# Setting the high and the low part of each channel block side by side in one tile

## The chip, the cores and the metric

The kernel runs on one core of one Trainium2 chip. The metric is the device time of one execution in microseconds (us). Three runs of the kernel before gave 1538.27, 1538.55 and 1540.19 us; their median, 1538.55 us, is the time that the change is measured against.

## The reference

Two stacks of layers are applied one after the other to one sequence of 256 tokens with 1024 channels, all in float32. The part that matters here is that nearly all the work is products of a normalised input with a weight matrix:

```
def first_block(x, ...):                 # 2 layers
    x = hybrid_layer(x, ...)             # h = rmsnorm(x); proj = h @ w_in (1024 x 2304)
                                         # two attentions; y = [rmsnorm(ya), rmsnorm(yb)]
                                         # x = x + y @ w_out (1024 x 1024)
                                         # u = rmsnorm(x) @ w_mlp_in (1024 x 4096); u = relu(u)^2
                                         # x = x + u @ w_mlp_out (4096 x 1024)
    return rmsnorm(x, final_norm)

def second_block(x, ...):                # 2 layers
    f = swiglu(x, w_gate, w_up, w_down)  # 1024 x 2816, 1024 x 2816, 2816 x 1024
    x = layer_norm(ALPHA * x + 0.5 * f)
    z = x @ w_in                         # 1024 x 2304, then three mixers
    x = layer_norm(ALPHA * x + y @ w_out)
    f = swiglu(x, ...); x = layer_norm(ALPHA * x + 0.5 * f)
```

## The kernel before

The channels lie across the 128 partitions in 8 blocks (`KT` = 8) and the 256 tokens in two tiles of 128 (`NT` = 2). A float32 product is made of three products of float32r operands: each operand is split into a high part (a copy rounded to float32r) and a low part (the remainder), and `mm3` (L165) adds high x high, high x low and low x high into one PSUM tile. So every line L166, L167 and L168 stands for one matmul of a triple.

A normalised input is kept transposed, with channels on partitions: `new_xT` (L103) gives two tiles, `xh` for the high and `xl` for the low part, each with 8 blocks of 256 tokens. `padded` (L73) makes such a tile 24 elements (96 bytes per partition) longer than its contents. The pool `xtp` has two buffers of each name, so that there are four tiles: `xh`, `xh`, `xl`, `xl`. The same pair holds the mixed output `yT` of an attention or of the mixers before its projection.

These tiles are written in pieces: by `transpose_to` and `split` (L224, L220: four blocks of 128 tokens in one instruction), by `rms_in` (L265 and L266: one block each), by `values` (L413 and L414: one block of 256 tokens) and in `mixers` by `split` from SBUF (two blocks of 256 tokens, L784 and L811). ACT writes the high part and DVE the low part.

They are read in three forms:

- `b_form` (L176): the weights, `whi` and `wlo`, are loaded into the array as the stationary operand, 128 columns at a time, and a whole block of `xh` or `xl` (256 tokens) streams through as the moving operand. One pass is 8 blocks x 3 matmuls = 24 matmuls of 256 columns.
- `a_form` (L170): `xh` or `xl` (128 tokens) is the stationary operand and 256 columns of `whi` or `wlo` stream. It is used in `layer1` throughout and elsewhere for the first units of a stage.
- `out_form` (L186): the stationary operand is a hidden activation in tiles of the name `six`, or `yT` in `xh` and `xl`; 512 columns of the weights stream.

The weights come by DMA into `wraw` (L148) and are split at L153 into `whi` (ACT) and `wlo` (DVE), with eight buffers each. Every stage begins with `enter` (L206), which sets the transposes of the new input between the last products of the stage before and the first of its own. The order of the attention stages is written out in `ORDER` (L39); in the rest it is the order of the code.

Of the kernel before, what the change touches and what calls it, by code (L numbers as in the profile page):

```python
# [12 lines left out]
F32R = mybir.dt.float32r  # L13
# [6 lines left out]
P = 128  # L20
S = 256
NT = 2
D = 1024
KT = 8
# [21 lines left out]
def hybrid_stack(ctx: ExitStack, tc: tile.TileContext, a, out):  # L46
# [7 lines left out]
    xtp = ctx.enter_context(tc.tile_pool(name="xtp", bufs=2))  # L54
# [15 lines left out]
    def T(pool, shape, tag, dt=F32, **kw):  # L70
        return pool.tile(shape, dt, tag=tag, name=nm(tag), **kw)

    def padded(pool, shape, tag, dt, **kw):  # L73

        n = shape[1] * shape[2]
        t = T(pool, [P, n + 24], tag, dt, **kw)
        return t[:, :n].rearrange("p (a b) -> p a b", b=shape[2])
# [23 lines left out]
        return [[acc1() for _ in range(2)] for _ in range(NT)]  # L101

    def new_xT():  # L103
        return padded(xtp, [P, KT, S], "xh", F32R), padded(xtp, [P, KT, S], "xl", F32R)

    def chunks():
        return [(c, slice(c * 512, (c + 1) * 512)) for c in range(2)]
# [336 lines left out]
    def layer1(l, xT, rx, boundary):  # L444
# [12 lines left out]
        kTB = T(m4k, [P, 4, S], "m4k")  # L457
        ssum = [T(tmp, [P, S], "ti", bufs=2) for _ in range(2)]
        yT = new_xT()
        rqA = T(tiny, [P, 16], "rqA", bufs=1).rearrange("p (t h) -> p t h", t=NT)  # L460
        held = {}
# [232 lines left out]
    def mixers(l, xT, boundary):  # L694
# [27 lines left out]
        for t in range(NT):  # L722
            alpha_x(t)
        yT = new_xT()


# [93 lines left out]
    acc, finish, r = None, None, None  # L820
    for l in range(DEPTH):
        xT = new_xT()
        if l == 0:
            tab = T(const, [P, NT, 160], "tab")
# [24 lines left out]
        xT = new_xT()  # L849
# [10 lines left out]
    xT = new_xT()  # L860
# [4 lines left out]
    def ln_stage(l, i, acc, scale):  # L865
        g, b = gain(a["ln_g_2"][l, i]), gain(a["ln_b_2"][l, i], tag="b")
        xT = None if (l, i) == (DEPTH - 1, 2) else new_xT()

        def f(t):
            ln_xT(x[t], acc[t], scale, g, b, xT, t, out[0, t * P:(t + 1) * P, :] if xT is None else None)  # L870

        return f, xT

    for l in range(DEPTH):
        acc, finish = ffn(l, 0, xT, (finish, norm))
        norm, xT = ln_stage(l, 0, acc, 0.5)
        acc, finish = mixers(l, xT, (finish, norm))
        norm, xT = ln_stage(l, 1, acc, 1.0)
        acc, finish = ffn(l, 1, xT, (finish, norm))
        norm, xT = ln_stage(l, 2, acc, 0.5)  # L880
# [73 lines left out]
```

## Time and profile before

| | |
|---|---|
| median of three runs | 1538.55 us |
| the profiled execution's own time | 1543.87 us |
| its span, first to last instruction | 1542.1 us |
| granted TensorE clock, mean over the span | 0.997 |
| busy: PE, PEld, DVE, ACT, POOL | 98%, 90%, 66%, 53%, 4% of the span |
| DMA | 177 GB/s in the mean |

PE stands for the matmuls, PEld for the loads of the stationary operand, which overlap with them; DVE, ACT and POOL are the engines for vector, scalar and general work. The matmuls are pipelined: the duration shown for one (some 280 ns for 256 columns) is longer than the distance between the starts of two, so what a matmul costs is read from the length of a stretch divided by the matmuls that begin in it. The profiled execution took 1.8 us outside its span.

### The profile page before, as it was taken

What the parts mean: (1) busy time and instruction counts of PE and PEld (TensorE: products, weight loads), DVE (VectorE), ACT (ScalarE), POOL (GpSimd) and SP (SyncE); (2) the same over time, 40 slices, a digit from 0 to 9 for tenths busy, and PEclk for the clock granted to TensorE, in tenths of its full rate; (3) what the DMA queues carried; (4) which work ended last, traced back from release to release, by engine and by line L of the source; (5) the groups of instructions that cost most, each with busy time, mean ns of one, the idle gap of its engine ahead of it and who ended that gap; (6) DMA issues with size and microseconds to landing.
All of it is one profiled execution on the core that took longest, in us unless ns stands there. A gap on an engine that the chain in (4) does not pass through costs nothing. (4 is left out here: it accounts for less than half of the span.)

```text
span 1542.1 us, 26996 instructions
## 1 busy us (share of the span) xinstructions
PE 1511.1 (98%) x10480; PEld 1390.8 (90%) x10480; DVE 1016.2 (66%) x2056; ACT 817.1 (53%) x1636; POOL 64.7 (4%) x94
## 2 busy tenths in 40 slices
PE   7999999999999999999999999999999999999998
PEld 6889999889899998999999899998999999899997
DVE  7977656589775555655577875556755477875554
ACT  6866554478574544544446554443644447454441
POOL 3000000030000000000000100000000000000000
PEclk9999999999999999999999999999999999999999
DMA  6624665635366654866646576664866646476661
GB/s 194 191 68 152 214 195 181 191 98 169 108 194 183 194 184 137 252 189 185 189 134 219 157 231 182 190 190 137 253 191 191 186 134 214 150 242 186 188 186 47
DMA packets 196368, 272.98 MB, mean 177 GB/s; under 512 B 9312, under 2 KB 169600, under 8 KB 196240
## 3 DMA queue, kind: packets, MB, share of 16 engines
q1 hardware_dynamic: 193664, 262.76, 55.6%
q0 software_dynamic: 2576, 8.50, 1.9%
q8 instruction: 82, 1.34, 0.4%
q14 instruction: 46, 0.38, 0.1%
HBM read 270.17 MB, written 1.05 MB: 176 GB/s over the span
## 5 line engine op out<-in xcount | busy, mean ns | idle before, releaser
L153 DVE TENSOR_TENSOR wlo<-wraw,whi 128x512 fp32r<-128x512 f32 x992 | 641.0, 687 | 363.6 <-ACT whi L153 354.6
L153 ACT CAST whi<-wraw 128x512 fp32r<-128x512 f32 x992 | 565.5, 619 | 530.6 <-issue 267.5
L166 PE MATMUL rot<-xh,whi 128*128 128x256 f32 x1088 | 306.3, 282 | 0.0
L167 PE MATMUL rot<-xl,whi 128*128 128x256 f32 x1088 | 306.1, 281 | 0.0
L168 PE MATMUL rot<-xh,wlo 128*128 128x256 f32 x1088 | 304.5, 280 | 0.0
L167 PE MATMUL aux<-xl,whi 128*128 128x256 f32 x864 | 242.5, 281 | 0.0
L166 PE MATMUL aux<-xh,whi 128*128 128x256 f32 x864 | 242.1, 280 | 0.0
L168 PE MATMUL aux<-xh,wlo 128*128 128x256 f32 x864 | 241.8, 280 | 0.0
L166 PE MATMUL acc<-whi,six 128*128 128x512 f32 x608 | 240.8, 396 | 0.2 <-ACT six L221 0.2
L168 PE MATMUL acc<-whi,six 128*128 128x512 f32 x608 | 238.8, 394 | 0.0
L167 PE MATMUL acc<-wlo,six 128*128 128x512 f32 x608 | 238.6, 393 | 0.0
L167 PEld LDWEIGHTS rot<-xl,whi 128*128 128x128 f32 x1088 | 204.6, 188 | 0.7
L166 PEld LDWEIGHTS rot<-xh,whi 128*128 128x128 f32 x1088 | 204.6, 188 | 0.6
L168 PEld LDWEIGHTS rot<-xh,wlo 128*128 128x128 f32 x1088 | 204.6, 188 | 0.1
L166 PEld LDWEIGHTS aux<-xh,whi 128*128 128x128 f32 x864 | 162.5, 188 | 2.1
L167 PEld LDWEIGHTS aux<-xl,whi 128*128 128x128 f32 x864 | 162.3, 188 | 2.2
L168 PEld LDWEIGHTS aux<-xh,wlo 128*128 128x128 f32 x864 | 162.5, 188 | 0.0
L166 PE MATMUL rot<-whi,xh 128*128 128x256 f32 x544 | 156.5, 288 | 0.6 <-ACT qk L719 0.5
L167 PE MATMUL rot<-wlo,xh 128*128 128x256 f32 x544 | 154.5, 284 | 0.8 <-DVE wlo L153 0.8
L168 PE MATMUL rot<-whi,xl 128*128 128x256 f32 x544 | 154.5, 286 | 0.1
L168 PEld LDWEIGHTS acc<-whi,six 128*128 128x128 f32 x608 | 114.1, 188 | 28.0 <-DVE six L222 1.0
L166 PEld LDWEIGHTS acc<-whi,six 128*128 128x128 f32 x608 | 114.2, 188 | 24.2 <-ACT six L221 1.7
(215 smaller groups left out, 1721.2 us busy)
## 6 DMA issues: line engine op xcount, KB each, us to landing
wraw<-in_ffn_w_gate_dram SPq DMA_DIRECT2D x88, 512.0 KB, 4.5
wraw<-in_ffn_w_up_dram SPq DMA_DIRECT2D x88, 512.0 KB, 4.4
wraw<-in_ffn_w_down_dram SPq DMA_DIRECT2D x88, 512.0 KB, 4.4
wraw<-in_w_in_dram SPq DMA_DIRECT2D x71, 512.0 KB, 4.6
wraw<-in_w_mlp_in_dram SPq DMA_DIRECT2D x64, 512.0 KB, 4.5
wraw<-in_w_mlp_out_dram SPq DMA_DIRECT2D x64, 512.0 KB, 4.5
wraw<-in_w_out_dram SPq DMA_DIRECT2D x32, 512.0 KB, 4.0
g<-in_ln_g_dram POOLq DMA_DIRECT2D x6, 512.0 KB, 4.1
```

Source lines behind the costliest of these rows:

```text
L153: done[:] = [se.copy(h, r), ve.tensor_tensor(l, r, h.bitcast(F32), op=ALU.subtract)]
L166: pe.matmul(o, lh, rh, start=first, stop=False)
L167: pe.matmul(o, lh, rl, start=False, stop=False)
L168: pe.matmul(o, ll, rh, start=False, stop=last)
```

## The change

`new_xT` now makes one tile, `xT`, of 16 blocks of 256 elements, and gives its even blocks as the high and its odd blocks as the low part:

```
     def new_xT():
-        return padded(xtp, [P, KT, S], "xh", F32R), padded(xtp, [P, KT, S], "xl", F32R)
+
+        xT = padded(xtp, [P, 2 * KT, S], "xT", F32R).rearrange("p (k i) s -> p k i s", i=2)
+        return xT[:, :, 0], xT[:, :, 1]
```

Nothing else is edited; lines behind L104 have a number higher by two. On every engine the built program has the same instructions in the same order, with the same waits. Two things differ.

First, the places. Within a partition the tiles before start at bytes 104768 and 113056 (`xh`) and 121344 and 129632 (`xl`), which is 320, 416, 512 and 608 bytes past a multiple of 1024; all of `whi` and `wlo` start 320 bytes past one. The new tiles start at 104768 and 121248, and the low block of a pair 1024 bytes behind the high one, so that high and low both lie 320 bytes past a multiple of 1024 in the first buffer and both 416 in the second. Since there are two pads fewer, every tile of the pools opened behind `xtp` starts 192 bytes earlier: the five `six` buffers were 0, 96, 192, 288 and 384 bytes past a multiple of 1024 and are now 832, 928, 0, 96 and 192. Tiles of pools opened earlier, `wraw`, `whi` and `wlo` among them, stay where they were.

Second, the shape of twelve writes. The two blocks that `split` writes in one instruction in `mixers` were adjacent and counted as one run of 512 elements; now a low block stands between them. On ACT, in the mixers of the first layer of the second block, where `whi` is a weight's high part and `m4k` and `six` are results of the mixers, there stood before:

```order
L774 COPY six_9869<-rot_9954 128x512 [waits PE_49]
L153 CAST whi_10173<-wraw_10172 128x512
L221 CAST xh_9488<-m4k_9491 128x512 [waits DVE_49,Activation_49]
L221 CAST xh_9488<-m4k_9491 128x512 [waits DVE_49]
L153 CAST whi_10181<-wraw_10180 128x512 [waits DMAHW2_49,PE_49]
L153 CAST whi_10181<-wraw_10180 128x512
```

and now:

```order
L776 COPY six_9860<-rot_9945 128x512 [waits PE_49]
L155 CAST whi_10164<-wraw_10163 128x512
L223 CAST xT_9480<-m4k_9482 128x2x256 [waits DVE_49,Activation_49]
L223 CAST xT_9480<-m4k_9482 128x2x256 [waits DVE_49]
L155 CAST whi_10172<-wraw_10171 128x512 [waits DMAHW2_49,PE_49]
L155 CAST whi_10172<-wraw_10171 128x512
```

The two casts write two runs of 256 in place of one of 512, at the same place in ACT's order and behind the same waits; a third cast some instructions later, and DVE's three subtractions for them, change in the same way, in each of the two layers.

On PE, at the first product of the program, the triple read two tiles:

```order
L166 MATMUL rot_227<-whi_162,xh_109 128x256 [waits Activation_49]
L262 MATMUL aux_271<-ident_99,x_188 128x128
L167 MATMUL rot_227<-wlo_163,xh_109 128x256 [waits DVE_49]
L168 MATMUL rot_227<-whi_162,xl_110 128x256
L166 MATMUL rot_227<-whi_162,xh_109 128x256
```

and reads one now:

```order
L168 MATMUL rot_225<-whi_160,xT_109 128x256 [waits Activation_49]
L264 MATMUL aux_269<-ident_99,x_186 128x128
L169 MATMUL rot_225<-wlo_161,xT_109 128x256 [waits DVE_49]
L170 MATMUL rot_225<-whi_160,xT_109 128x256
L168 MATMUL rot_225<-whi_160,xT_109 128x256
```

No matmul moved, and none waits for anything that it did not wait for before.

## Rows read from the trace of the kernel before

**Rows 1.** The page: span, busy time by engine, granted clock in 40 slices.
```profile
span 1542.1 us, 26996 instructions
...
PE 1511.1 (98%) x10480; PEld 1390.8 (90%) x10480; DVE 1016.2 (66%) x2056; ACT 817.1 (53%) x1636; POOL 64.7 (4%) x94
...
PEclk9999999999999999999999999999999999999999
```

**Rows 2.** The page: the chain that ended last, by engine.
```profile
DVE 0%; DVEq 0%; issue 0%
```

**Rows 3.** Waits of PE, the two longest: us in total, times, longest.
```profile
PE aux L262 <- DMA x<-in_x_dram: 9.3, 2, 5.0
PE aux L355 <- DVE four L222: 2.8, 2, 2.0
```

**Rows 4.** Groups by form: count, busy us and mean ns, idle before.
```profile
L153 DVE TENSOR_TENSOR wlo<-wraw,whi 128x512 fp32r<-128x512 f32 x992 | 641.0, 687 | 363.6 <-ACT whi L153 354.6
L153 ACT CAST whi<-wraw 128x512 fp32r<-128x512 f32 x992 | 565.5, 619 | 530.6 <-issue 267.5 <-PE rot L167 91.9 <-PE acc L168 79.1
L166 PE MATMUL rot<-xh,whi 128*128 128x256 f32 x1088 | 306.3, 282 | 0.0
...
L166 PE MATMUL aux<-xh,whi 128*128 128x256 f32 x864 | 242.1, 280 | 0.0
...
L166 PE MATMUL acc<-whi,six 128*128 128x512 f32 x608 | 240.8, 396 | 0.2 <-ACT six L221 0.2
...
L166 PE MATMUL rot<-whi,xh 128*128 128x256 f32 x544 | 156.5, 288 | 0.6 <-ACT qk L719 0.5
...
L166 PE MATMUL acc<-whi,xh 128*128 128x512 f32 x128 | 51.9, 405 | 0.0
```

**Rows 5.** PE by window, matmuls reading `xh`: length, busy (count), clock, DMA share, GB/s.
```profile
704.77:716.08 11.31, 11.31 (x64) 1.00 0.60 185
926.75:938.05 11.31, 11.31 (x64) 1.00 0.61 191
```

**Rows 6.** PE by window, matmuls writing `acc`: four groups of 24 with `six`.
```profile
171.80:177.31 5.51, 5.51 (x24) 1.00 0.72 210
194.16:199.75 5.59, 5.59 (x24) 1.00 0.65 196
182.97:188.51 5.54, 5.54 (x24) 1.00 0.70 215
...
536.61:542.10 5.50, 5.50 (x24) 1.00 0.70 212
```

**Rows 7.** PE by window, matmuls writing `acc`: two groups of 24 with `yT`.
```profile
862.25:867.84 5.58, 5.58 (x24) 1.00 0.71 224
...
1323.16:1328.71 5.55, 5.55 (x24) 1.00 0.75 229
```

**Rows 8.** PE by window, matmuls writing `rot`: three passes of `a_form`.
```profile
68.76:71.59 2.83, 2.83 (x26) 1.00 0.39 146
65.85:68.76 2.91, 2.91 (x24) 1.00 0.73 218
379.11:381.88 2.77, 2.77 (x26) 1.00 0.03 6
```

**Rows 9.** Groups by form: writes of `xh` and `xl` by `split`.
```profile
L222 DVE TENSOR_TENSOR xl<-aux,xh 128x512 fp32r<-128x512 f32 x24 | 15.7, 686 | 2.4 <-ACT xh L221 2.3
...
L221 ACT CAST xh<-aux 128x512 fp32r<-128x512 f32 x24 | 14.1, 588 | 59.6 <-PE aux L227 58.7
...
L222 DVE TENSOR_TENSOR xl<-m4k,xh 128x512 fp32r<-128x512 f32 x4 | 2.6, 682 | 0.0
...
L221 ACT CAST xh<-m4k 128x512 fp32r<-128x512 f32 x4 | 2.3, 621 | 2.1 <-DVE m4k L810 2.1
...
L222 DVE TENSOR_TENSOR xl<-aux,xh 128x256 fp32r<-128x256 f32 x4 | 1.7, 421 | 0.1
...
L221 ACT CAST xh<-aux 128x256 fp32r<-128x256 f32 x4 | 1.5, 366 | 0.0
```

## The prediction

> **What bounds the kernel now.** I read the page first. Its busy shares show one engine that never rests: PE is busy for 1511.1 of 1542.1 us, DVE for 66% and ACT for 53% [rows 1]. The granted clock stands at nine tenths or more in each of the 40 slices [rows 1], so the clock hides nothing and has nothing to give back; it is at the upper of its two levels, 2.4 GHz. The chain that ended last has 0% for each engine that it names [rows 2], because it only follows the last few microseconds of the program; it is no guide here, and I went to the waits instead. PE's longest waits are 9.3 us for the first load of `x` and 2.8 us in an attention [rows 3]. In the groups the idle time ahead of the matmuls is between 0.0 and 0.6 us over hundreds of instructions, while DVE and ACT wait hundreds of microseconds ahead of the weights' splits [rows 4]. So the kernel takes as long as PE needs to work off its matmuls one after the other, and the only question about a change is whether it makes a matmul start later after the one before it.
>
> **What a matmul costs** is the length of a stretch divided by the matmuls in it. Two stretches of four `b_form` passes, one on the first and one on the second buffer of the input, both take 11.31 us [rows 5]. The rows count 64 matmuls that read `xh`; with one on `xl` for every two of these it is 96, so 11.31 / 96 = 117.8 ns each. With `six` as the loaded operand, 24 matmuls of 512 columns take 5.50, 5.51, 5.54 or 5.59 us [rows 6], which is 229.2 to 232.9 ns each; with `yT` 5.55 and 5.58 us [rows 7]. A pass of `a_form` takes 2.83, 2.91 or 2.77 us for the 24 matmuls that begin in it (the rows' counts take in the tail of a neighbour) [rows 8].
>
> The counts come from the groups, three lines to a form [rows 4]: `b_form` has 3 x (1088 + 864) = 5856 matmuls, or 690 us; `a_form` 3 x 544 = 1632, which is 68 passes, or 192 us; `out_form` with `six` 3 x 608 = 1824, which is 76 groups of 24, or 421 us at 5.54; with `yT` 3 x 128 = 384, which is 16 groups, or 89 us. These are 1392 of the 1542 us.
>
> **The change, part by part.** Instructions, order and waits are the same on every engine, so nothing is removed, added or queued behind something else. No DMA of a weight lands elsewhere. What remains is where operands lie.
>
> *Twelve writes in two runs.* In the mixers six casts on ACT take 621 ns and six subtractions on DVE 682 ns for one run of 512 [rows 9]. The nearest rows are the same two lines writing four runs of 128: 588 and 686 ns [rows 9], so runs by themselves cost nothing on either engine (the first reads from another memory, so I use it for the order of size only). The far bound is that two runs of 256 cost as much as two instructions of 256: 2 x 366 = 732 and 2 x 421 = 842 ns [rows 9], which is 6 x 0.11 + 6 x 0.16 = 1.6 us in all. I take the four-run rows, hence 0. Even the far bound would lie beside PE's work: before the casts of weights ACT is idle for 530.6 us in total and DVE for 363.6 us [rows 4]. With that cover gone it would be +1.6 us.
>
> *`b_form`.* The weights are loaded and the input streams. The loaded operand stays at its place. What streams moves: a low block lay 512 or 608 bytes past a multiple of 1024 and now lies 320 or 416 past one, as the high block does and did. The two buffers before differ in just this, by 96 bytes in both parts, and their stretches agree to the last digit shown, 0.01 us in 11.31 [rows 5]. So I take 0, with 61 such stretches x 0.01 = 0.6 us to either side as far as offsets like those seen go.
>
> *`out_form` with `six`.* Here the loaded operand moves by 192 bytes, and this is where the trace does show a dependence: the groups of [rows 6] have the same code, the same engines and the same clock, and differ in which of the five buffers hold the high and the low part. The fast ones, 5.51 and 5.50 us, have the high part at offset 0 and the low at 384; the slow one, 5.59, at 192 and 0; the one between, 5.54, at 288 and 96. DMA traffic does not explain it, since a fast and a slow group have 210 and 196 GB/s. The change gives all five buffers new offsets, so each pair draws anew. I find no rule in the rows that tells good offsets from bad ones: 288 and 96 are as far apart as 192 and 0. The middle of the ends, 5.545, is my value before and after, so 0; the ends are 76 x 0.045 = 3.4 us either way.
>
> *`a_form` and `yT`.* The loaded operand is `xh` or `xl`. Its low part moves from 512 or 608 to 320 or 416. Of the three passes the usual one is 2.83; 2.91 is the first pass behind transposes, in either buffer, and I read it as their tail rather than as an offset; 2.77 is rare. I take 2.83, so 0. The ends are 68 x 0.06 = 4.1 us down and, if 2.91 were an offset after all, 68 x 0.08 = 5.4 us up. For `yT` it is 16 x 0.03 = 0.5 us.
>
> The sum is 0. With all ends at once it is -8.6 or +11.5 us, but these are draws for ten or so pairs of buffers and three forms, and they partly cancel; a third of the ends, -3 to +4 us, is my own range for the sum.
>
> **A rule of the Trainium skill against these rows.** The Trainium skill, in "TensorE: Matmul & The Clock Gate", section "Back-to-back issue gap", gives N / 2.4 + 2.5 ns between matmuls of N columns, and in "What happens when you issue a matmul" it says that the loads have a read port of their own, so that they take nothing from the running matmul. By that, as an estimate from this page, 256 and 512 columns would take 109 and 216 ns and no offset could matter; the sum would be 0 with no ends at all. The trace disagrees in both: 117.8 ns [rows 5], and 229.2 to 232.9 ns by buffer [rows 6]. I go by the rows, which leave the sum where it is and give it its ends.
>
> **From the profiled execution to the median.** The rows are of an execution of 1542.1 us span and 1543.87 us in all, 5.3 us above the median of 1538.55. A difference of 0 carries over to the median as it is: **1538.5 us**. A measurement of this kernel tells a difference from none at about 0.2%, which is 3.1 us.
>
> **The rivals.**
>
> *Slower: high, low and weights in step.* In the first buffer every streamed block and every loaded block of `b_form` now have the same offset, 320, and in the second 416 against 320, without exception. If PE reads the streamed and the loaded operand from one memory and they get in each other's way when in step, the third of `b_form` that streams `xl` would pay. The price from the rows is the slow against the fast group, (5.59 - 5.50) / 24 = 3.75 ns [rows 6]; 1952 matmuls x 3.75 ns = +7.3 us, hence 1545.9 us. It decides from the point where a stretch of 96 takes over 11.36 us (+3.1 us over 61 stretches). Against it speaks that in the first buffer before two of three matmuls were in step already, in the second none, and both took 11.31 us [rows 5]. I give it 0.10; together with a bad draw of `six` and `a_form` by over 3.1 us, slower has 0.15.
>
> *Faster: a good draw.* If most pairs of `six` land where 5.50 is, that is -3.4 us, and if equal offsets of high and low bring `a_form` to 2.77, -4.1 us [rows 6, 8]; both are 1531.0 us, and one of them with a little of the other some 1534.5 us. For it: two of the four groups in the rows are already at 5.50. Against it: these are averages over many pairs, and a pair that is fast now loses its place too. I give it 0.12.
>
> *The change does not do what it says*, because high and low part in one tile might be taken for one piece of memory, with reads of the one waiting for writes of the other. The PE rows of the order show no wait added, and PE waits 0.0 us at nearly all triples [rows 4]; under 0.01.
>
> **How the numbers follow.** No change beyond 0.2% has 0.73, faster 0.12, slower 0.15. The forecast's own range is 1535.5 to 1542.5 us. To leave out no more than two in ten I reach to the near edge of both draws, 1534.5 and 1543.0 us; the in-step case at 1545.9 stays outside.
>
> **What would show it.** Right: a `b_form` stretch of four passes at 11.31 us in both buffers, twelve writes near 621 and 682 ns, groups with `six` still between 5.50 and 5.59 us but in another order of buffers, `a_form` passes at 2.83. Wrong: a `b_form` stretch off 11.31 by 0.05 or more, since 5856 matmuls hang on it; all groups of `six` at one end; or a new wait of PE of over 3 us.

## The result, and the profile after

The changed kernel takes 1551.14 us in the median of six runs, the kernel before, in six runs too, 1540.04 us. The ratio is 1.0073, with a 95% interval of 1.0061 to 1.0084: 11.1 us slower, outside the range of the prediction.

On the page of the profile after, the span and PE's busy time answer to [rows 1]:

```profile
span 1549.4 us, 26996 instructions
...
PE 1521.8 (98%) x10480; PEld 1402.2 (91%) x10480; DVE 1015.7 (66%) x2056; ACT 817.0 (53%) x1636; POOL 64.6 (4%) x94
```

PE is busy for 10.7 us longer with the same number of instructions; DVE, ACT and POOL are not. The span grew by 7.3 us only, because PE idled 27.6 us in this execution and 31.0 in that of before. About half of that lies at the first transposes, on which no part of the change acts. There PE waited 9.3 us before, in two waits for the loads of `x` [rows 3]. In the waits of PE after (us in total, times, longest) the second of the two is put down to a split of a weight, and both together are 7.6 us:

```profile
PE aux L264 <- DMA x<-in_x_dram: 4.0, 1, 4.0
PE aux L264 <- DVE wlo L155: 3.6, 1, 3.6
```

Behind the first transposes no wait of PE grew by more than 0.7 us, so it is not waits that make the kernel slower. What grew is the distance between matmuls. Two stretches of four `b_form` passes, on the first and on the second buffer, with the matmuls on `xT` counted (the second count takes in the tail of a neighbour), answer to [rows 5]:

```profile
654.79:666.30 11.52, 11.52 (x96) 1.00 0.62 187
816.94:828.46 11.52, 11.52 (x98) 1.00 0.89 284
```

They took 11.31 us and take 11.52, which is 120.0 ns for a matmul in place of 117.8, at a granted clock of 1.00 as before. If all 61 stretches were like these two, it would be 61 x 0.21 = 12.8 us. Groups of 24 that write `acc` answer to [rows 6, 7]; the first three load `six`, the last two `yT`:

```profile
157.76:163.37 5.61, 5.61 (x24) 1.00 0.81 275
169.12:174.67 5.55, 5.55 (x24) 1.00 0.67 214
191.75:197.25 5.49, 5.49 (x24) 1.00 0.66 206
864.06:869.51 5.45, 5.45 (x24) 1.00 0.76 231
869.51:874.95 5.44, 5.44 (x25) 1.00 0.58 167
```

With `six` these groups spread from 5.49 to 5.61 us, about as before; with `yT`, whose parts now have equal offsets too, they became faster, 5.44 in place of 5.55 us. Passes of `a_form` answer to [rows 8]:

```profile
66.94:69.82 2.88, 2.88 (x26) 1.00 0.54 152
376.91:379.72 2.81, 2.81 (x26) 1.00 0.02 6
63.98:66.94 2.96, 2.96 (x24) 1.00 0.81 227
```

Each of these three is 0.04 or 0.05 us longer than the pass at its place before. The twelve writes in two runs answer to [rows 9], in groups by form, for eight of the twelve:

```profile
L224 DVE TENSOR_TENSOR xT<-m4k,xT 128x512 fp32r<-128x512 f32 x4 | 2.6, 684 | 0.0
L223 ACT CAST xT<-m4k 128x512 fp32r<-128x512 f32 x4 | 2.3, 621 | 1.9 <-DVE m4k L812 1.9
```

They take 684 and 621 ns, as one run did (682 and 621).

### The profile page after: what moved, and what is told of

It is laid out like the page before. It is cut to its first block, busy times and chain, and to the rows that moved or that the text cites. A ratio compares the mean times of both kernels' runs of the same rounds, so it can differ in the third digit from the quotient of the medians.

```text
span 1549.4 us, 26996 instructions
## 1 busy us (share of the span) xinstructions
PE 1521.8 (98%) x10480; PEld 1402.2 (91%) x10480; DVE 1015.7 (66%) x2056; ACT 817.0 (53%) x1636; POOL 64.6 (4%) x94
## 5 line engine op out<-in xcount | busy, mean ns | idle before, releaser
L168 PE MATMUL rot<-xT,whi 128*128 128x256 f32 x1088 | 308.6, 284 | 0.0
L169 PE MATMUL rot<-xT,whi 128*128 128x256 f32 x1088 | 308.0, 283 | 0.0
L170 PE MATMUL rot<-xT,wlo 128*128 128x256 f32 x1088 | 307.1, 282 | 0.0
L169 PE MATMUL aux<-xT,whi 128*128 128x256 f32 x864 | 244.2, 283 | 0.0
L170 PE MATMUL aux<-xT,wlo 128*128 128x256 f32 x864 | 244.0, 282 | 0.0
L168 PE MATMUL aux<-xT,whi 128*128 128x256 f32 x864 | 243.8, 282 | 0.0
L169 PEld LDWEIGHTS rot<-xT,whi 128*128 128x128 f32 x1088 | 206.1, 189 | 0.8
L168 PEld LDWEIGHTS rot<-xT,whi 128*128 128x128 f32 x1088 | 206.2, 190 | 0.6
L170 PEld LDWEIGHTS rot<-xT,wlo 128*128 128x128 f32 x1088 | 206.3, 190 | 0.1
L168 PEld LDWEIGHTS aux<-xT,whi 128*128 128x128 f32 x864 | 163.9, 190 | 2.2
L169 PEld LDWEIGHTS aux<-xT,whi 128*128 128x128 f32 x864 | 163.6, 189 | 2.2
L170 PEld LDWEIGHTS aux<-xT,wlo 128*128 128x128 f32 x864 | 164.0, 190 | 0.0
L168 PE MATMUL rot<-whi,xT 128*128 128x256 f32 x544 | 156.1, 287 | 0.5 <-ACT qk L721 0.5
L169 PE MATMUL rot<-wlo,xT 128*128 128x256 f32 x544 | 154.2, 284 | 0.7 <-DVE wlo L155 0.6
L170 PE MATMUL rot<-whi,xT 128*128 128x256 f32 x544 | 154.2, 285 | 0.7 <-DVE xT L268 0.6
```

Of the source, the lines that this page charges most:

```text
L168: pe.matmul(o, lh, rh, start=first, stop=False)
L169: pe.matmul(o, lh, rl, start=False, stop=False)
L170: pe.matmul(o, ll, rh, start=False, stop=last)
```

## The experiments

Theory 1 was that `b_form` is slow because the high and the low block, which stream one after the other, have the same offset. Its rivals were the neighbourhood (one tile, a step of 2048 bytes between blocks) and the 192 bytes by which all later tiles moved. Each stretch shown below is four passes of `b_form`, 96 matmuls, unless the text says otherwise; the count in brackets is of the matmuls on the tile named `xh` (64 of the 96) or `xT` (96).

**Equal offsets in two separate tiles.**

```
-        return padded(xtp, [P, KT, S], "xh", F32R), padded(xtp, [P, KT, S], "xl", F32R)
+        return (T(xtp, [P, KT, S], "xh", F32R), T(xtp, [P, KT, S], "xl", F32R))
```

and a filler of 384 bytes behind them.

> The kernel before with two separate tiles for high and low part, but without their pads, so that all four start 320 bytes past a multiple of 1024 and a low block has the same offset as its high block; a filler keeps every other tile where it was before. Theory 1 (equal offsets of the high and the low block that stream one after the other cost it): a stretch of 96 b_form matmuls takes 11.52 us instead of 11.31, and the kernel is about 11 us (0.7%) slower than before. Theory 2 (the neighbourhood costs it: blocks 1024 bytes apart in one tile, a step of 2048 between blocks): 11.31 us and the time of before. Theory 3 (the 192 bytes by which the other tiles moved cost it): the time of before.

It took 1550.76 us, a ratio to before of 1.0074 (1.0058 to 1.0090), and in its trace:

```profile
671.29:682.79 11.50, 11.50 (x64) 1.00 0.61 189
```

This is the change's loss without the change's layout. The neighbourhood is not needed for it.

**Side by side with 32 bytes between.**

```
-        xT = padded(xtp, [P, 2 * KT, S], "xT", F32R).rearrange("p (k i) s -> p k i s", i=2)
-        return xT[:, :, 0], xT[:, :, 1]
+        t = T(xtp, [P, KT * 520], "xT", F32R).rearrange("p (k n) -> p k n", n=520)
+        return t[:, :, 0:S], t[:, :, 264:264 + S]
```

> The changed kernel with high and low block still side by side in one tile, but with 32 bytes behind each block, so that a low block starts 1056 bytes behind its high block (32 past the same offset) and the next high block another 1024 on. Theory 1: offsets differ again, so a stretch of 96 b_form matmuls comes back to about 11.31 us and the kernel to within 0.3% of before, if 32 bytes are enough of a difference. Theory 2: still 11.5 us and about 0.7% slower than before. Theory 3: still slower, since the other tiles moved too.

It took 1543.61 us, a ratio of 1.0024 (1.0015 to 1.0033):

```profile
654.44:665.77 11.34, 11.34 (x96) 1.00 0.63 188
815.23:826.57 11.34, 11.34 (x98) 1.00 0.93 287
```

With the high and low block still neighbours in one tile, 0.18 of the 0.21 us came back, and two thirds of the time. The rest of 0.24% is not all explained by 61 x 0.03 = 1.8 us. The 32 bytes stand behind each high block only; so every pair of blocks lies 32 bytes further past a multiple of 256 than the one before it, and the tiles behind `xtp` lie 128 bytes later than in the kernel before.

**The change, with the rest in place.** A filler of 192 bytes behind `xtp`:

```
+    fill = ctx.enter_context(tc.tile_pool(name="fill", bufs=1))
+    fill.tile([P, 48], F32, tag="fill", name="fill")
```

> The changed kernel with a filler of 192 bytes behind its input tiles, so that every other tile lies where it lay before. Theories 1 and 2: nothing comes back in b_form, 11.52 us for 96 matmuls; groups of six return to 5.50 to 5.59 us as before; 0.6 to 0.8% slower than before. Theory 3: the time of before.

It took 1552.02 us, a ratio of 1.0078 (1.0061 to 1.0095), and `b_form` stays slow, so the moved tiles are not the cause:

```profile
656.21:667.71 11.50, 11.50 (x96) 1.00 0.65 187
```

One part of the expectation failed. These are the groups of 24 with `six` that stand where [rows 6] stand, with the same buffers at the same addresses as before:

```profile
170.62:176.22 5.60, 5.60 (x24) 1.00 0.71 217
181.96:187.51 5.55, 5.55 (x24) 1.00 0.70 203
193.27:198.87 5.60, 5.60 (x24) 1.00 0.71 221
```

The group that took 5.51 us before, high part at offset 0 and low at 384, takes 5.60 here. The time of such a group hangs on more than its own addresses; what differs in the matmuls ahead of it is the place of the low part in `b_form`.

**How large a difference must be.** With two tiles, the low part 128, 256, 512 or 64 bytes past the offset of the high one (a pool of its own for `xl` behind a gap of so many bytes, both parts without pads, the rest in place but for 512, where it lies 128 bytes later). The cut is of the first, without its filler and its line in `new_xT`:

```
+    gap = ctx.enter_context(tc.tile_pool(name="gap", bufs=1))
+    gap.tile([P, 32], F32, tag="gap", name="gap")
+    xlp = ctx.enter_context(tc.tile_pool(name="xlp", bufs=2))
```

> The kernel before with all high tiles 320 bytes past a multiple of 1024 and all low tiles 128 bytes further, every other tile in place. Theory 1a (only equal offsets modulo 1024 cost): 11.31 us for a stretch of 96 b_form matmuls, as with a difference of 192. Theory 1b (the offsets count modulo 128 or less): 11.52 us, as with no difference.

> The same with the low tiles 256 bytes further than the high ones. Theory 1a: 11.31 us. Theory 1b, modulo 128 or 256: 11.52 us. If 128 bytes gave 11.31 and this gives 11.52, the length is 256.

> The same with the low tiles 512 bytes further than the high ones (the tiles behind them lie 128 bytes later). Theory 1a: 11.31 us. Theory 1b, modulo 512 or a divisor of it: 11.52 us.

> The kernel before with all high tiles 320 bytes past a multiple of 1024 and all low tiles 64 bytes further. Equal offsets modulo 256 cost 11.52 us in a stretch of 96 b_form matmuls, 32, 128 and 192 bytes gave 11.31 to 11.35. If only a difference of 0 modulo 256 is bad: 11.31 us.

With 128 bytes:

```profile
634.16:645.47 11.31, 11.31 (x64) 1.00 0.82 260
```

with 256:

```profile
708.87:720.37 11.50, 11.50 (x64) 1.00 0.60 185
```

with 512:

```profile
656.64:668.15 11.50, 11.50 (x64) 1.00 0.61 188
```

and with 64:

```profile
636.06:647.37 11.31, 11.31 (x64) 1.00 0.86 261
```

The single times agree: 1537.97, 1554.52, 1552.54 and 1541.37 us, against runs of the kernel before between 1537 and 1545. Theory 1a falls, and so does 1b for 128: of the differences tried, 0, 256 and 512 are bad and 32, 64, 128 and 192 are not, so the offsets of the streamed pair count modulo 256 bytes, and 0 is the bad difference.

**Is it the streamed pair alone?** The changed kernel with the pool `wlo` 128 bytes later, so that the loaded pair `whi`, `wlo` has unequal offsets (all tiles behind, the input's among them, lie 128 bytes later too):

```
+    gapw = ctx.enter_context(tc.tile_pool(name="gapw", bufs=1))
+    gapw.tile([P, 32], F32, tag="gapw", name="gapw")
     wlo = ctx.enter_context(tc.tile_pool(name="wlo", bufs=8))
```

> The changed kernel (high and low block of the input equal modulo 256) with all wlo tiles 128 bytes further from whi modulo 256. Theory 1 as it stands (the streamed pair alone decides): b_form stays at 11.52 us for 96 matmuls and the kernel 0.6 to 0.8% slower than before. Theory 1c (both the streamed pair and the loaded pair must be equal for the slow pace): b_form comes back to about 11.31 us and the kernel to within 0.3% of before.

It took 1543.06 us, a ratio of 1.0018 (1.0009 to 1.0028):

```profile
652.23:663.59 11.36, 11.36 (x96) 1.00 0.64 195
813.09:824.46 11.37, 11.37 (x98) 1.00 0.98 307
```

Theory 1 as it stood falls and 1c holds: the slow pace needs equal offsets in both pairs. Shifting the weights' low part gives most of the loss back, though the input's parts are still equal. That the input's tiles moved along was not tried by itself; in the changed kernel its two buffers lie at different offsets against the weights, and both take 11.52 us. The 0.05 us left of a stretch, 61 times, are 3 us, as much as the kernel's 0.18%.

**Equal offsets for `six`.** In the kernel before, the five `six` buffers without pads, all at 0:

```
-        return padded(tmp, shape, "six", dt, bufs=5)
+        return T(tmp, shape, "six", dt, bufs=5)
```

> The kernel before with the pads of the five six buffers taken away, so that high and low part of a hidden activation have equal offsets when they are loaded as the stationary operand of out_form; the input tiles stay as before. In the changed kernel the groups of 24 that load yT from the input tiles went from 5.55 to 5.44 us when its parts got equal offsets. If that holds for six (theory 1 for loads, with the other sign): groups of 24 near 5.44 instead of 5.50 to 5.59 us, 76 of them, about 8 us (0.5%) faster than before. If equal offsets cost there as they do in b_form: about 4 us slower. If offsets of loads are a draw without a rule: within 3 us of before.

It took 1537.81 us, a ratio of 0.9987 (0.9976 to 0.9998). None of the three cases fits whole: the time is within 3 us of before, as in the third, but the groups no longer spread. All that no wait disturbs were at the fast end of [rows 6], not at 5.44:

```profile
169.15:174.66 5.50, 5.50 (x24) 1.00 0.72 230
487.12:492.62 5.50, 5.50 (x24) 1.00 0.67 206
```

**The same at the weights' offset, 320.** `six` gets a pool of its own ahead of `tmp`, behind a filler.

> The kernel before with the five six buffers without pads and all 320 bytes past a multiple of 1024, the offset of whi and wlo; in the equal-offset run before this they were all at 0 and a group of 24 took 229.1 x 24 = 5.50 us. With yT at the weights' own offset, groups took 5.44 us in the changed kernel. If being in step with the streamed weights is what gives 5.44: groups of six at 5.44 us, 76 x 0.12 = 9 us less than before, 0.6% faster. If only high against low counts: 5.50 us, 76 x 0.06 = 4.5 us less than before at most, 0.1 to 0.3% faster.

It took 1535.33 us, a ratio of 0.9965 (0.9955 to 0.9975), and is faster than both kernels:

```profile
169.37:174.83 5.46, 5.46 (x24) 1.00 0.71 227
487.96:493.49 5.53, 5.53 (x24) 1.00 0.69 208
```

The first group, behind a first-buffer `b_form`, came near the 5.44 us, the second, behind a second-buffer one, did not. It is so for nearly every group that no wait disturbs: 5.46 us in the three stages whose `b_form` reads the first buffer, 5.53 in the three that read the second, with `six` at one offset in both. The size lies between the two expected cases.

**`six` in step, and `wlo` 128 bytes away** (the two edits together):

> The kernel with six in step, and besides all wlo tiles 128 bytes further from whi modulo 256 (the tiles behind them lie 128 bytes later). In out_form the streamed pair whi and wlo now has unequal offsets and the loaded pair equal ones, as b_form has before. In b_form both pairs are unequal. If the rule of b_form holds for any streamed pair (equal offsets cost): groups of six under 5.44 us and the kernel over 0.6% faster than before. If equal streamed and equal loaded offsets are what made 512 columns cheap: groups of six go up to 5.50 us or more. For b_form, if only the streamed pair counts: 11.31 us; anything else shows that the loaded pair counts too.

It took 1538.35 us, a ratio of 0.9988 (0.9978 to 0.9997). In its `b_form` stretches, first and second buffer:

```profile
651.15:662.45 11.30, 11.30 (x64) 1.00 0.61 185
811.70:822.94 11.24, 11.24 (x65) 1.00 0.95 303
```

and in two groups with `six`:

```profile
169.57:175.12 5.55, 5.55 (x24) 1.00 0.66 223
488.58:494.18 5.60, 5.60 (x24) 1.00 0.70 217
```

Unequal streams did not help 512 columns; they lost what equal offsets had given. In `b_form` the second buffer gained another 0.07 us and the first did not, so the loaded pair has a part there too, and with it where the buffer lies.

**The change, with `six` in step**, so that all triples of these three forms are equal in both pairs:

> The changed kernel with the five six buffers without pads and all at offset 320, so that every triple of b_form, a_form and out_form has equal offsets in the loaded and in the streamed pair. Theory 1c: b_form stays at 11.52 us for 96 matmuls (120.0 ns each). In out_form the equal offsets gave 226.7 ns with yT in the changed kernel and 229.4 with six where b_form before it had unequal offsets. If a fixed distance between matmuls is carried from one form into the next, groups of six now take 226.7 x 24 = 5.44 us throughout, 76 x 0.13 = 10 us less than in the changed kernel, and the kernel is within 0.3% of before. If the 229.4 belonged to the six tiles: 5.51 us, 0.3 to 0.6% slower than before.

It took 1546.25 us, a ratio of 1.0034 (1.0022 to 1.0045), with 11.51 and 11.52 us for the stretches and, for two groups with `six`:

```profile
171.73:177.20 5.47, 5.47 (x24) 1.00 0.65 214
491.76:497.25 5.48, 5.48 (x24) 1.00 0.63 204
```

The groups are even, and faster than the 5.49 to 5.61 of the changed kernel, but not 5.44 throughout; they lie between the two expected cases. The ratio lies in the second, at its near edge. That a distance is carried from one form into the next is only half supported.

The traces of all runs together say more than the two groups shown of each. Over the 64 or 65 groups with `six` that no wait disturbs, the mean is 5.47 to 5.50 us in the three runs where the parts of `six` and the parts of the weights are both equal, and 5.55 to 5.57 us in every other run, the one with `wlo` moved included.

## Why the prediction was wrong

**The bound was right.** PE's matmuls in a row set the time: PE's busy time grew by 10.7 us where the medians differ by 11.1, behind the first transposes no wait grew by more than 0.7 us, and DVE, ACT and POOL are busy as long as before, within 0.5 us.

**The step that failed is the term of `b_form`**, taken as 0 with 0.6 us to either side. It measured +11.7 us: in the 240 of its 244 passes that no wait disturbs in either trace, the mean went from 2.832 to 2.881 us (61 x 0.21 = 12.8 us, from the two stretches shown, is a little high). Its argument was that the two buffers before differ in just what the change changes, "by 96 bytes in both parts". They do not. In both, the low part lay 192 bytes past the offset of the high one; by comparing them I had tested where the pair lies against the weights, which does not matter in these two kernels (11.52 us in both buffers after, at 320 and at 416, and 11.31 in both before; with `wlo` moved and `six` in step the two buffers do differ, 11.30 and 11.24). What the change changes is the distance within the pair, and of that the kernel before had a single value. No row could bound it, and I wrote a bound as if one did.

**The rival "in step"** had the right sign, a size of the right order (+7.3 us against 11.1) and a point of decision, 11.36 us, that the trace crossed. Its mechanism was wrong in part: it set the streamed against the loaded operand and charged a third of the matmuls 3.75 ns, while all three of a triple pay, 1.3, 2.2 and 2.7 ns in the means of the two traces; and what the runs show to be slow is high and low part at equal offsets among the streamed and among the loaded. The argument by which I gave it 0.10, that two of three matmuls were in step before, belongs to the wrong version of it.

**The other terms.** The writes cost 0, as taken. For the matmuls I added up, in both traces, the time from the start of each to the start of the next, waits included: `b_form` went from 695.4 to 705.5 us, `a_form` from 211.7 to 211.9, `out_form` with `six` from 424.8 to 425.5 and with `yT` from 90.9 to 90.0. That is +10.1 us, against 10.7 in PE's busy time and 11.1 in the medians, and `b_form` is all of it (its 11.7 less 1.6 us that four disturbed passes waited less). So the three passes of `a_form` shown above are no measure of all 68: the 45 that no wait disturbs in either trace grew by 0.026 us in the mean, and the disturbed ones shrank by nearly as much in all. With `yT` the gain of 0.9 us is beyond the end of 0.5 that I gave it. With `six` the new offsets were a draw that came out even: 65 undisturbed groups have a mean of 5.57 us, against 5.56 before. My claim there that the pair of buffers decides a group's time held inside one kernel but not across kernels (5.51 and 5.60 us at the same addresses). The upper end of my range, 1543.0 us, I had worked out from no row.

**The rule of the Trainium skill** that I weighed, in "TensorE: Matmul & The Clock Gate", section "Back-to-back issue gap", goes by the number of columns and would have given no effect at all; the runs have 117.8 and 120.0 ns for the same 256 columns. Going by the rows was right, and was not enough, since I let the rows speak only of the offsets that they contained.

## What to carry to other kernels

When operands move in memory, list every relation between them that the move alters (each against each, and modulo powers of two), and ask of each whether the trace holds two values of it; a relation with one value is not bounded, however steady its rows are. Split products that stream high and low parts through 256 columns did best here with the two parts unequal modulo 256 bytes, and through 512 columns with the parts equal in both operands. Removing the pads of the hidden activations and setting them at the weights' offset made this kernel 0.35% faster than before.

## What the runs showed of the hardware

- Where high and low part have equal offsets in the loaded and in the streamed pair of each triple, the distance between matmuls is 120.0 ns for 256 columns and, with `yT`, 226.7 ns for 512 (5.44 / 24). The 256 columns more cost 106.7 ns, which is one column per cycle of 2.4 GHz; at that pace 13.3 ns come on top of either. With `six` it was 227.5 to 230.4 ns in such layouts (5.46 to 5.53 us). Where one of the pairs is unequal, or both, it was 117.1 to 118.4 ns for 256 columns in the stretches shown and 229 to 233.5 for 512, which is 10 to 12 and 16 to 20 ns on top. So the same offsets are a loss for 256 columns and a gain for 512.
- For the streamed pair of `b_form` the period is 256 bytes: differences of 0, 256 and 512 gave 11.50 to 11.52 us, of 32, 64, 128 and 192 gave 11.31 to 11.34. Differences under 32 bytes were not run. For the loaded pair only equal offsets and a difference of 128 were, so its period is not shown.
- Why PE behaves so is open; no run here looks inside it. Why a group with `six` depends on the form ahead of it is open as well.
